# Down projections unit by unit, two-bank scores, a shorter last norm, and low parts of the first mixer's weights on VectorE

## The chip, the cores and the metric

The kernel runs on one core of a Trainium2 chip. The metric is device time in microseconds (us). Five engines work side by side, each in its own order of instructions: TensorE (PE: matmuls; PEld: its weight loads), VectorE (DVE), ScalarE (ACT), GpSimd (POOL) and SyncE (SP), which issues most of the transfers between device memory and the on-chip memory SBUF. Matmuls write PSUM, a small memory of eight banks, from which VectorE and ScalarE read.

## What is computed

The reference is a two-layer decoder trunk on one sequence of 1024 tokens with 1024 features, all in float32:

```python
def reference(x, ...):
    h = x
    for layer in range(DEPTH):                       # DEPTH = 2
        n = rms_norm(h, norm1_g[layer])
        if layer % 2 == 0:
            mix = retention_rwkv_mixer(n, ...)       # the first mixer: recurrences by chunks
        else:
            mix = swa_sink_mixer(n, ...)             # attention, 16 heads, window of 128
        h = h + mix
        n = rms_norm(h, norm2_g[layer])
        h = h + swiglu(n, ffn_w_gate[layer], ffn_w_up[layer], ffn_w_down[layer])
    return rms_norm(h, final_g)

def swiglu(h, w_gate, w_up, w_down):
    return (jax.nn.silu(h @ w_gate) * (h @ w_up)) @ w_down      # 1024 -> 2816 -> 1024
```

In attention, a block of 128 queries sees its own 128 keys and the 128 before them: scores, plus a band mask, a softmax with one learned extra term, and a weighted sum of values.

## The kernel before, in words

**Layout.** Features lie on the 128 partitions: `h` is 8 tiles of 128 features for each half of the tokens (`hf` 0 and 1, 512 tokens each, `HT`). A matmul has a 128x128 weight and 512 tokens.

**Three matmuls for one.** A float32 product is made of three faster ones. Each operand is split into a high part (a rounding cast on ScalarE) and a low part (operand minus high part, a subtraction on VectorE or GpSimd); then hi·hi, hi·lo and lo·hi are added in PSUM: `gemm` (L342-348) and, for the feed-forward part, `prod` (L1174-1179), where L1177, L1178 and L1179 are the three matmuls. The splits are `wsplit` (weights; cast L331, subtraction L332 on the engine `self.lo`, which is GpSimd unless set otherwise), `split` (activations; L352 cast, L354 subtraction) and `vsplit` (weights of the down projection; cast L1350, subtraction on GpSimd L1351). So no product starts before both parts of its weights and inputs are there. Split weights go through six buffers (`w` four, `wr` two).

**Who sets the order.** The kernel is written as a program over tiles. A scheduler then sets the order of the instructions on each engine, by its own model of their times; instructions that are given to `keep` hold their place in the program's order on their engine. Buffers come from named pools with a fixed number of each; a tile waits until the buffer's last user is done.

**The run.** First mixer with its output projection (a planner runs generators of jobs, `pl.run()`; for the first half of the tokens the weights are split and written back to memory, for the second the split weights are read), feed-forward part of layer 0, attention, feed-forward part of layer 1, final norm. The hidden features of the feed-forward part are made in 11 pairs of 256 (`NP`); a step of each pair ends in the gates (Silu on ScalarE, L1224) and the product with the up projection (L1228 on VectorE). Hidden tiles go to device memory (`hid`), and so do sums of them (`hc`), made by `form_down` (its `put` subtracts, L1304, splits and writes them).

**Down projection** (`down`, L1380 on). It is a two-by-two block product by seven products in place of eight (Strassen's way, in Winograd's form). In layer 0, 8 of the 11 pairs go through it in two groups of four slices (`DGROUPS`), the rest plainly; in layer 1 all 11 do, in groups of four, four and three. A group has seven stages s0 to s6. In a stage, one input X (hidden tiles, read from `hid` and split, or sums, read from `hc` split) meets four weights `W[dp]`, one for each of four PSUM banks: four units of 12 matmuls (9 in the group of three). Between them stand sums of weights (`wsum`: three for each `dp` in s0, one in s2) and additions of results to `h`, all on VectorE at L1377. Copies of results are at L1411 on ScalarE. The order of s0's units, the next input's split and the sums is the scheduler's. The first group's loads and splits come after the last pair of the feed-forward part has been written in program order, in pools (`fa`, `fz`) that open when the others close.

**Attention** (`attn`). 32 blocks of 128 queries for four heads at a time. The heads of a pair lie on partitions 0 to 63 and 64 to 127. For each row half `e`, two score matmuls (L1552, 64 rows of weights) go to a PSUM bank of their own, `r` or `c`, and VectorE adds the mask (L1556, 512 elements) into `s`; then maxima (L1562), exponentials on ScalarE (L1569), normalising (L1575), transposes on TensorE (L1582), copies (L1584 on ScalarE, L1586 on VectorE) and the product with the values (L1592). Projections of the feed-forward part (L346-348) run between.

**Final norm.** `final_r` (L1623 on): for each of the eight tiles a square and a copy scaled by the gain, both on ScalarE; sums of squares on VectorE (L1627) and over partitions by a matmul with ones (L1629); logarithm and exponential on ScalarE (L1631, L1632), each with a table load. `final_out` multiplies (L1639, VectorE and GpSimd) and writes the output (L1640). For the first half of the tokens `final_r` runs before the last two stages of the last group.

Of the kernel before, what the change touches and what calls it, by code (L numbers as in the profile page):

```python
# [13 lines left out]
ALU = mybir.AluOpType  # L14
# [190 lines left out]
class Kern:  # L205
    def __init__(self, ctx, tc, A, out):
# [15 lines left out]
        self.wx = None  # L222
        self.w6, self.nw, self.owed, self.lo = False, 0, [], self.nc.gpsimd
# [168 lines left out]
    def mixer0(self):  # L392
# [54 lines left out]
        jobs(1, "ret", (1, 2, 3))  # L447
        pl.run()
        gr.__exit__(None, None, None)
# [767 lines left out]
    def uses(self, L, p, sp, x=None):  # L1217
# [4 lines left out]
        def gate(nm, c):  # L1222
            sg[nm] = self.t(sp, [P, HT], "sg", 2) if nm == "11" else c
            S.activation(sg[nm], c, AF.Silu)  # L1224
# [61 lines left out]
    def ffn_pair(self, L, p, sp, next_w, form, x):  # L1286
# [10 lines left out]
        self.lockstep(*gens, form)  # L1297

    def form_down(self, L, p, x, ts):
# [3 lines left out]
        def put(i, o, a, b):  # L1303
            nc.vector.tensor_tensor(out=o, in0=a, in1=b, op=ALU.subtract)  # L1304
# [40 lines left out]
    def vsplit(self, v):  # L1345
# [4 lines left out]
        nc.scalar.copy(hi, v)  # L1350
# [29 lines left out]
    def down(self, L, fp, fz, rest, X=()):  # L1380


        op, S = self.vop, self.nc.scalar
        h0, h1 = (self.kt(self.h[hf]) for hf in range(2))
        dps = range(KT // 2)
        j = len(X)

        def place():
            nonlocal j
            i, j = j % (12 if L else 14), j + 1  # L1390
            if i >= 8 if L else i < 6:
                return self.t(fp, [P, 2, HT], "ha", 4 if L else 6, F32R)
            return self.t(self.pp, [P, 2, HT], "n8", 8, F32R)

        def plain(hf, f):
            return self.plain8(L, hf, f, place(), self.t(fp, [P, HT], "hr", 4))

        for g in DGROUPS[L]:
            n, ps = g[1] - g[0], range(*g)
            s1, u0 = [], []  # L1400
            W = [self.wdown(L, 0, g, fp, "wd0", 5)]
            X = X or [plain(0, 2 * p) for p in ps]
            W += [self.wdown(L, 2 * i, g, fp, "wd0", 5) for i in (1, 2, 3)]
            for i in dps:
                W[i] += self.wdown(L, 2 * i + 1, g, fp, "wd1", 6 - L)
            A = [self.pst(t, [P, HT]) for t in "fffy"]
            for dp in dps:
                a11, a12, a21, a22 = W[dp]
                self.prod(A[dp], self.vsplit(a11), X, True, False)
                u0.append(self.t(fz, [P, HT], "u0", 4))  # L1410
                S.copy(u0[dp], A[dp])  # L1411
                s1.append(op(self.wsum(fp, n, 4, 8), a21, a22))
                op(a21, a11, a21, ALU.subtract)
                W[dp][0] = op(self.wsum(fp, n, 4, 8), s1[dp], a11, ALU.subtract)
            X = [self.sums8(L, p, 2, place()) for p in ps]
# [18 lines left out]
            for _ in rest:  # L1434
                pass
# [398 lines left out]
```

## Time and profile before

| what | value |
|---|---|
| time, median of 3 runs | 2391.7 us (2388.97 to 2393.98) |
| the profiled execution | 2394.0 us, of which the span from first to last instruction is 2392.2 us |
| mean granted TensorE clock | 0.992 |
| TensorE busy | 2318.9 us (97%) |
| VectorE, GpSimd, ScalarE busy | 1626.3, 1193.1, 1025.5 us (68, 50, 43%) |
| down projection of layer 0, 1140 to 1340 us | TensorE 194.4 of 200 us busy, VectorE 134.3, GpSimd 139.8 |
| down projection of layer 1, 2140 to 2380 us | TensorE 231.0 of 240 us busy, VectorE 175.6, GpSimd 160.9 |

A row of the timeline gives the start, the duration, the engine, the line and operation, the tile written and those read, and a count; what stands in brackets is the engine's idle time before it and the instruction that ended the idle time. A row "x4" is four instructions in a row, with their time together. A row of a window gives its length, the busy time (and count) of PE, PEld, DVE, ACT and POOL, the granted clock, the DMA engines' busy share and GB/s. A row of groups gives busy time in all and mean ns of one, then the idle time before them and what ended it. A row of waits gives time in all, how often, and the longest. Matmuls are pipelined: each record is longer than the distance to the next, so their pace is read from start to start.

### The profile page before, as it was taken

How to read it: one execution, taken by the hardware profiler on the slowest of the kernel's cores; microseconds unless marked ns; L12 is line 12 of the kernel's file. 1: busy time of each engine (PE TensorE's matmuls, PEld its weight loads, DVE VectorE, ACT ScalarE, POOL GpSimd, SP SyncE). 2: the span in 40 equal slices, each digit the busy share in tenths (PEclk: the TensorE clock that was granted, in tenths of full speed). 3: DMA queues.
4: the chain of work that ended last, by engine and by line, in shares of the span. 5: the costliest groups of instructions: out<-in, count | busy, mean ns of one | idle time of the engine just before them, and what ended most of it. 6: DMA issues, size and time to landing. Idle time of an engine off the chain costs nothing. (4 is left out here: it accounts for less than half of the span.)

```text
span 2392.2 us, 35667 instructions
## 1 busy us (share of the span) xinstructions
PE 2318.9 (97%) x13098; PEld 1828.7 (76%) x13098; DVE 1626.3 (68%) x2462; ACT 1025.5 (43%) x1890; POOL 1193.1 (50%) x975
## 2 busy tenths in 40 slices
PE   8999899999999999999999999999999999999997
PEld 6776677777777888888778877677788788887785
DVE  5865855765567368885775469458638778887776
ACT  5354443324456333333333555455645233333336
POOL 7555331211541057776676632342232677767666
PEclk9999999999999999999999999999999999999999
DMA  7655454443445556563564321231336466547652
GB/s 267 197 204 188 154 165 133 126 128 115 146 172 181 198 171 212 195 216 137 217 222 153 118 62 58 66 131 62 106 128 220 159 217 218 203 178 274 219 200 107
DMA packets 167742, 395.93 MB, mean 166 GB/s; under 512 B 42896, under 2 KB 45584, under 8 KB 167568
## 3 DMA queue, kind: packets, MB, share of 16 engines
q1 hardware_dynamic: 164448, 388.15, 47.8%
q10 hardware_dynamic: 2832, 4.45, 0.6%
q8 instruction: 104, 1.70, 0.3%
q0 software_dynamic: 288, 1.05, 0.1%
q14 instruction: 70, 0.57, 0.1%
HBM read 271.29 MB, written 116.92 MB: 162 GB/s over the span
## 5 line engine op out<-in xcount | busy, mean ns | idle before, releaser
L332 POOL TENSOR_TENSOR w<-wr,w 128x512 fp32r<-128x512 f32 x196 | 264.3, 1354 | 427.9 <-ACT w L331 369.9
L239 PE MATMUL ps_f<-n,w 128*128 128x512 f32 x1440 | 383.5, 414 | 12.0 <-ACT w L331 6.4
L239 PEld LDWEIGHTS ps_f<-n,w 128*128 128x128 f32 x1440 | 268.3, 192 | 93.3 <-issue 21.9
L331 ACT CAST w<-wr 128x512 fp32r<-128x512 f32 x244 | 147.9, 612 | 188.8 <-PE ps_f L348 76.9
L332 POOL TENSOR_TENSOR w<-wq,w 128x512 fp32r<-128x512 f32 x92 | 130.5, 1430 | 31.7 <-ACT w L331 27.4
L346 PE MATMUL ps_f<-n,w 128*128 128x512 f32 x356 | 140.8, 396 | 2.6 <-ACT n L352 1.6
L347 PE MATMUL ps_f<-n,w 128*128 128x512 f32 x356 | 142.6, 400 | 0.0
L348 PE MATMUL ps_f<-n,w 128*128 128x512 f32 x356 | 140.1, 394 | 0.0
L1177 PE MATMUL ps_f<-n,w 128*128 128x512 f32 x322 | 127.5, 397 | 4.1 <-DVE h L1377 1.8
L1184 DVE TENSOR_TENSOR nq<-ps_m,u 128x512 f32<-128x512 f32 x88 | 58.7, 684 | 106.7 <-PE ps_m L1179 106.7
L1178 PE MATMUL ps_f<-n,w 128*128 128x512 f32 x322 | 125.5, 390 | 0.0
L1179 PE MATMUL ps_f<-n,w 128*128 128x512 f32 x322 | 125.2, 390 | 0.0
L354 POOL TENSOR_TENSOR n<-nq,n 128x512 fp32r<-128x512 f32 x64 | 106.0, 1667 | 10.2 <-ACT n L352 10.2
L1177 PE MATMUL ps_m<-n,w 128*128 128x512 f32 x282 | 110.6, 393 | 0.0
L1179 PE MATMUL ps_m<-n,w 128*128 128x512 f32 x282 | 109.8, 389 | 0.0
L1178 PE MATMUL ps_m<-n,w 128*128 128x512 f32 x282 | 109.8, 389 | 0.0
L332 POOL TENSOR_TENSOR wx<-wr,wx 128x512 fp32r<-128x512 f32 (+1 forms) x38 | 49.4, 1301 | 105.5 <-ACT wx L331 105.5
L1177 PE MATMUL ps_m<-cb,w 128*128 128x512 f32 x240 | 93.5, 389 | 0.9 <-DVE nq L1184 0.9
L1178 PE MATMUL ps_m<-cb,w 128*128 128x512 f32 x240 | 93.4, 389 | 0.0
L1179 PE MATMUL ps_m<-cb,w 128*128 128x512 f32 x240 | 93.4, 389 | 0.0
L1351 POOL TENSOR_TENSOR w<-wd,w 128x512 fp32r<-128x512 f32 (+1 forms) x53 | 75.9, 1442 | 32.0 <-ACT w L1350 31.8
L346 PEld LDWEIGHTS ps_f<-n,w 128*128 128x128 f32 x356 | 66.9, 188 | 20.0 <-ACT n L1598 2.2
(520 smaller groups left out, 6447.6 us busy)
## 6 DMA issues: line engine op xcount, KB each, us to landing
hc<-n SPq DMA_DIRECT2D x74, 512.0 KB, 2.7
wsp<-w SPq DMA_DIRECT2D x54, 512.0 KB, 3.4
w<-wsp SPq DMA_DIRECT2D x54, 512.0 KB, 3.7
wq<-in_w_gate SPq DMA_DIRECT2D x44, 512.0 KB, 4.2
u<-u SPq DMA_DIRECT2D x88, 256.0 KB, 2.9
n<-hc SPq DMA_DIRECT2D x43, 512.0 KB, 5.1
wr<-in_w_in SPq DMA_DIRECT2D x34, 512.0 KB, 5.0
hid<-n SPq DMA_DIRECT2D x66, 256.0 KB, 2.0
```

Source lines behind the costliest of these rows:

```text
L239: i = self.nc.tensor.matmul(out, lhsT, rhs, **kw)
L331: nc.scalar.copy(hi[:, :n], raw[:, c])
L332: self.lo.tensor_tensor(out=lo[:, :n], in0=raw[:, c], in1=hi.bitcast(F32)[:, :n], op=ALU.subtract)
L346: nc.tensor.matmul(ps, hi, rh, start=k == 0, stop=False)
L347: nc.tensor.matmul(ps, hi, rl, start=False, stop=False)
L348: nc.tensor.matmul(ps, lo, rh, start=False, stop=k == n - 1)
L354: e.tensor_tensor(out=lo, in0=src, in1=hi.bitcast(F32), op=ALU.subtract)
L1177: mm(ps, hi, xh, start=first and k == 0, stop=False, skip_group_check=True)
L1178: mm(ps, hi, xl, start=False, stop=False, skip_group_check=True)
L1179: mm(ps, lo, xh, start=False, stop=last and k == len(w) - 1, skip_group_check=True)
L1184: add = lambda o, x, y: V.tensor_tensor(out=o, in0=x, in1=y, op=ALU.add)
L1351: nc.gpsimd.tensor_tensor(out=lo, in0=v, in1=hi.bitcast(F32), op=ALU.subtract)
```

## The change

**Down projections.** `down` is written anew as one sequence of units (stage, `dp`). For each unit the program has: what follows the unit before (`post`), the split of a weight three units ahead (`ready`), a piece of the next stage's input (`prep`), the sums (`sums`), the transfers of an input two stages ahead (`get`) and, in s3 and s5, the loads of the next group's weights. The instructions of these on VectorE and ScalarE are held in that order (`pin`). All low parts in it are made on VectorE (`halves`): 139 of weights and 53 of hidden tiles; 25 of the latter were on VectorE before. One, the first weight's of layer 1, stays on GpSimd.

**The way in.** The last step of the last pair of the feed-forward part is put off (`rest(last)`). In layer 0 the first loads, the first input's splits and the first weights' come ahead of it; in layer 1 the first weight's load and split do. The pool `fa` opens earlier for it. In layer 1 the last `form_down` runs at the end of s2 of the first group (it stood ahead of its sums).

On ScalarE at the way into layer 0's down projection, with gates `ACTIVATE nq` and `u`, hidden tiles `hr` into `ha` and weights `wd` into `w` and `wr`, there stood:

```order
L1224 ACTIVATE nq_10326<-nq_10326 128x512
L1224 ACTIVATE u_1527_10317<-u_1527_10317 128x512
L1224 ACTIVATE nq_10325<-nq_10325 128x512
L1350 CAST wr_10534<-wd_1543_10494 128x512
L352 CAST ha_10496<-hr_10497 128x512
L352 CAST ha_10501<-hr_10502 128x512
L352 CAST ha_10506<-hr_10507 128x512
L352 CAST ha_10511<-hr_10512 128x512
L1350 CAST w_10556<-wd_1552_10516 128x512
```

and now (L1424 is the cast in `halves`, L1228 the gate):

```order
L1228 ACTIVATE nq_10326<-nq_10326 128x512
L1424 CAST ha_10463<-hr_10464 128x512
L1424 CAST ha_10466<-hr_10467 128x512
L1424 CAST ha_10469<-hr_10470 128x512
L1424 CAST ha_10472<-hr_10473 128x512
L1424 CAST wr_10483<-wd_1543_10461 128x512
L1424 CAST w_10548<-wd_1553_10486 128x512
L1228 ACTIVATE u_1527_10317<-u_1527_10317 128x512
L1424 CAST w_10551<-wd_1554_10488 128x512
L1228 ACTIVATE nq_10325<-nq_10325 128x512
```

The four casts of hidden tiles and two of weights have moved ahead of the last two gates.

**Attention.** The scores of both row halves go to one tile of two banks (`rc`), the loop over the row half is the inner one, and one addition of 1024 elements takes the place of two of 512. On TensorE, two consecutive blocks of the first half of the tokens (`ps_r`, `ps_c` the scores, `ps_m` transposes, `ps_y` products with values, `ps_f` projections) stood so before:

```order
L1552 MATMUL ps_r_13141<-ks_1861_12217,q_1876_12306 128x256 x2
L1552 MATMUL ps_c_13145<-kc_1856_12181,q_1876_12306 128x256 x2
...
L1582 MATMUL ps_m_13014<-c_ident_150,s_12988 128x128 x4
L1552 MATMUL ps_r_13186<-ks_1861_12217,q_1876_12306 128x256 x2
L1582 MATMUL ps_m_13020<-c_ident_150,s_12988 128x128 x2
L1592 MATMUL ps_y_12893<-pT_12886,vt_12220 64x256 x2
L1582 MATMUL ps_m_13020<-c_ident_150,s_12988 128x128 x2
L1552 MATMUL ps_c_13190<-kc_1856_12181,q_1876_12306 128x256 x2
```

and a block stands so now (L1665 the scores, L348 and L350 projections, L1706 the product with values):

```order
L1706 MATMUL ps_y_13010<-pT_12997,vt_12228 64x256 x3
L350 MATMUL ps_f_13549<-n_1843_12143,wx_13543 128x512
L1665 MATMUL ps_rc_13209<-ks_1861_12225,q_1876_12314 128x256
L1665 MATMUL ps_rc_13209<-kc_1856_12189,q_1876_12314 128x256
L1665 MATMUL ps_rc_13209<-ks_1861_12225,q_1876_12314 128x256
L1665 MATMUL ps_rc_13209<-kc_1856_12189,q_1876_12314 128x256
L348 MATMUL ps_f_13481<-n_1844_12144,w_13478 128x512
```

The four matmuls of a block stand together, the row halves in turn, where one block in the rows before had other work between them.

**First mixer.** While the planner runs, `wsplit` makes its low parts on VectorE: 66 instructions go there from GpSimd. VectorE's order near the start had additions `z` (L624) and the mixing with the token before (L627) right behind the norm (L463, L526):

```order
L463 SCALAR_TENSOR_TENSOR n_40_167<-r_22_137,pv_66,n_36_163 128x512
L526 TENSOR_TENSOR nq_204<-nq_201,nq_204 128x512
L624 TENSOR_TENSOR z_256<-ps_f_219,rs_237 128x512
L627 SCALAR_TENSOR_TENSOR wa_255<-wa_255,pv_66,z_256 128x512
L624 TENSOR_TENSOR z_297<-ps_f_271,rs_237 128x512
```

and has now low parts (L334) between them:

```order
L467 SCALAR_TENSOR_TENSOR n_40_167<-r_22_137,pv_66,n_36_163 128x512
L334 TENSOR_TENSOR w_263<-wr_139,w_263 128x512
L530 TENSOR_TENSOR nq_204<-nq_201,nq_204 128x512
L334 TENSOR_TENSOR w_266<-wr_139,w_266 128x512
L334 TENSOR_TENSOR w_305<-wr_269,w_305 128x512
L334 TENSOR_TENSOR w_309<-wr_269,w_309 128x512
L334 TENSOR_TENSOR w_347<-wr_313,w_347 128x512
L628 TENSOR_TENSOR z_256<-ps_f_219,rs_237 128x512
```

Five low parts of weights that TensorE uses for later tiles have come ahead of the first `z`.

**Final norm.** The scaled copies on ScalarE are gone; `final_out` multiplies by gain and factor in one instruction, always on VectorE. The logarithm's table is loaded in the stream, squares of the second half are made as its tiles are finished (`final_after`), and two of the first half's outputs are made in the last stage.

The diff, cut to its core:

```diff
+        self.lo = nc.vector
         pl.run()
+        self.lo = nc.gpsimd
...
-            S.activation(sg[nm], c, AF.Silu)
+            i = S.activation(sg[nm], c, AF.Silu)
+            if self.hold:
+                self.keep(i)
...
+    def pin(self, i):
+        k = str(i.ins.engine)
+        if k in self.pins:
+            self.tc.add_manual_dep(i.ins, self.pins[k], self.nosync, reason="order")
+        self.pins[k] = i.ins.name
+        return i
...
+        def halves(o, t, src):
+            pin(S.copy(t[0], src))
+            pin(V.tensor_tensor(out=t[1], in0=src, in1=t[0].bitcast(F32), op=ALU.subtract))
+            o.append((t[0], t[1]))
...
+        for i, (si, dp) in enumerate(units):
+            gi, s = gs(si)
+            if i:
+                k = self.done(post, L, *gs(units[i - 1][0]), units[i - 1][1])
...
+            while len(ready) < 3 and i + len(ready) < len(units):
+                u, v = units[i + len(ready)]
+                if gs(u)[1] == 0 or True:
+                    ready.append(split(part(*gs(u), v)))
+            if si + 1 < len(stages):
+                prep(si + 1, dp)
+            sums(gi, s, dp)
+            if i and k is not None:
+                self.final_after(k)
+            if self.outs and s == 6 and dp > 1:
+                next(self.outs)
+            if si + 2 < len(stages):
+                get(si + 2, dp)
+            if gi + 1 < len(DGROUPS[L]):
+                if s == 3:
+                    load(gi + 1, dp)
+                if s == 5:
+                    load(gi + 1, dp + 4)
+            if gi == 0 and s == 2 and dp == 3:
+                while self.owed:
+                    self.keep(self.nc.sync.dma_start(*self.owed.pop(0)))
+                for _ in rest:
+                    pass
+            ps = banks[gi, "ABABBCC"[s]][dp]
+            self.prod(ps, ready.popleft(), XS[si], s in (0, 1, 5), s in (2, 4, 6))
...
-                for e in range(2):
-                    ps = self.pst("rc"[e], [P, 2, 256])
...
+                ps = self.pst("rc", [P, 2, 2, 256])
+                for i in range(2):
+                    for e in range(2):
...
-            nc.scalar.activation(h(k), h(k), AF.Copy, scale=self.col("nf", k))
...
+                nc.vector.scalar_tensor_tensor(
+                    out=h(k), in0=h(k), scalar=self.col("nf", k), in1=r, op0=ALU.mult, op1=ALU.mult
+                )
...
+        last = ffn_late(0, sp, K.pp, opened)[3]
+        close(gb)
         gf, fp = K.pool("fa", "left")
+        fs = [fp]
+        f = K.down(0, fs, ())
+        next(f)
+        rest(last)
...
         r0 = K.final_r(0, fz, order[0], 7)
+        K.keep(tc.nc.scalar.preload_act_table(AF.Ln))
+        K.outs = K.final_out(0, r0, order[0])
         run(f)
-        r1 = K.final_r(1, fz, order[1], 4)
-        K.final_out(0, r0, order[0], "pppppppp")
-        K.final_out(1, r1, order[1], "vpvvpvvp")
+        r1 = K.final_r1(fz)
+        run(K.outs)
+        run(K.final_out(1, r1, order[1]))
```

259 lines of the change are left out of this document (174 added, 85 removed).

## The prediction

> **What bounds the kernel now.** I began with the page's busy times, then the windows of 20 and 30 us, then what TensorE waited for in each stage, and last the timeline at those waits.
>
> ```profile
> PE 2318.9 (97%) x13098; PEld 1828.7 (76%) x13098; DVE 1626.3 (68%) x2462; ACT 1025.5 (43%) x1890; POOL 1193.1 (50%) x975
> ...
> 2310.00:2340.00 30.00, 30.00 (x134) 24.86 (x133) 17.12 (x21) 13.70 (x26) 16.15 (x17) 1.00 0.55 184
> 1180.00:1200.00 20.00, 20.00 (x90) 16.56 (x89) 10.70 (x15) 4.35 (x7) 15.47 (x11) 1.00 1.02 390
> 0.00:300.00 300.00, 277.08 (x2129) 210.45 (x2130) 205.40 (x371) 141.48 (x225) 162.10 (x183) 0.98 0.60 202
> ```
>
> TensorE is busy for 97% of the span, and the change removes hardly any of its work, so a gain can only come from its holes and from the ends. Where nothing waits, 90 matmuls of 512 columns fill 20 us: one starts every 0.222 us. The two down projections are such stages with holes in them. These rows are TensorE's waits of 1140 to 1340 us (first five) and of 2140 to 2380 us (last five):
>
> ```profile
> PE ps_f L1178 <- POOL ha L354: 2.1, 1, 2.1
> PE ps_r L1177 <- ACT wr L1350: 1.4, 1, 1.4
> PE ps_y L1177 <- DVE h L1377: 1.1, 1, 1.1
> PE ps_f L1177 <- DVE h L1377: 0.6, 1, 0.6
> PE ps_m L1179 <- POOL wr L1351: 0.2, 1, 0.2
> ...
> PE ps_f L1177 <- DVE h L1377: 3.1, 3, 1.6
> PE ps_f L1179 <- POOL wr L1351: 1.8, 1, 1.8
> PE ps_y L1177 <- ACT w L1350: 0.9, 1, 0.9
> PE ps_f L1178 <- POOL ha L354: 0.8, 1, 0.8
> PE ps_f L1177 <- ACT w L1350: 0.7, 1, 0.7
> ```
>
> That is 5.4 us in layer 0 and 7.3 us in layer 1. The timeline at the first of them shows why:
>
> ```profile
> 1148.28 0.63 ACT L1224 ACTIVATE nq<-nq 128x512 f32<-128x512 f32 x1 [5.18 <-DVE nq L1184]
> ...
> 1149.33 2.17 ACT L352 CAST ha<-hr 128x512 fp32r<-128x512 f32 x4
> 1150.74 3.46 POOL L354 TENSOR_TENSOR ha<-hr,ha 128x512 fp32r<-128x512 f32 x2
> 1156.49 1.67 DVE L1377 TENSOR_TENSOR wd<-wd,wd 128x512 f32<-128x512 f32 x1
> 1159.78 0.68 DVE L1377 TENSOR_TENSOR ws<-wd 128x512 f32<-128x512 f32 x1
> 1168.50 0.63 PE L1177 MATMUL ps_m<-ha,wr 128*128 128x512 f32 x1
> ...
> 1171.06 0.63 PE L1179 MATMUL ps_r<-ha,wr 128*128 128x512 f32 x1
> ```
>
> ScalarE cannot cast the first halves before the last gate has run (1148.28 us), and only then does GpSimd begin its low parts at 1.73 us each (3.46 for two). Beside them the same kind of subtraction on VectorE takes 1.67 us instead of 0.68, so both chains are late for the second stage too. After such a hole TensorE goes at half pace for a while: the last two rows are the first and the last of seven matmuls that start (1171.06 − 1168.50) / 6 = 0.427 us apart, and layer 1 has seven such too; 7 × (0.427 − 0.222) = 1.4 us each. Measured from start to start, with 0.222 us taken off, all stops come to another 1.9 and 2.0 us, since a restart is slower than the wait shown and some stops are too short for the list. So the down projections lose 5.4 + 1.4 + 1.9 = **8.7 us** (layer 0) and 7.3 + 1.4 + 2.0 = **10.7 us** (layer 1).
>
> **Part 1: the way into the down projections.** In layer 0 the hid halves and first weights come ahead of the last gates, in layer 1 the first weight does. The casts then run while TensorE still has the last products to do, and VectorE makes a low part in 0.68 us. A unit of 12 matmuls lasts 12 × 0.222 = 2.67 us, and the low parts for the next one need 0.7 us each, so after the first unit VectorE keeps ahead. So the 2.1, 1.4 and 0.2 us of layer 0 go, and the 1.8 and 0.8 us of layer 1, with the slow clock after them. What is late next is the second stage's transfers, which are issued no earlier than now; what they may cost is in the residual below. In layer 1 VectorE has these on its way as well:
>
> ```profile
> 2152.85 1.64 DVE L1304 TENSOR_TENSOR n<-n,n 128x512 f32<-128x512 f32 x1
> ```
>
> Four such subtractions (some 6.6 us) stand ahead of the first sums now, and go to the end of the third stage. Their four splits and two transfers to memory go with them. They are needed only in the third group, more than one group of 75 us later, so this move is costed at nothing; if the transfers were late after all, the third group would wait. It puts 4 × 0.68 = 2.7 us on VectorE at that place, about one unit, out of a lead of two units.
>
> **Part 2: the steady down projections.**
>
> ```profile
> 2242.60 0.68 DVE L1377 TENSOR_TENSOR h<-h,ps_f 128x512 f32<-128x512 f32 x1
> 2243.20 0.68 DVE L1377 TENSOR_TENSOR ws<-wd,ws 128x512 f32<-128x512 f32 x1
> ```
>
> The waits on `h` (0.6, 1.1 and 3.1 us) are late writers of a PSUM bank behind the slow sums, and those on ACT `w` (0.9, 0.7) are casts that stood behind other waits. With GpSimd silent, VectorE's instructions should all take the 0.68 us of the row above. What VectorE then has to do: 92 instructions in a group of four slices, × 0.68 = 63 us, against 28 units × 2.67 = 75 us of TensorE. It fits. In the first two stages of a group it is 4 × 0.68 = 2.72 us against 2.67, which the lead absorbs. In the last group of layer 1 (three slices, units of 2.0 us, 56 us) it is about full: 28 low parts and 16 sums of 384 columns at 0.55, 9 hid halves, 36 additions and some 12 of the norm at 0.68, two outputs at 0.75: 24 + 39 + 1.5 = 64 us by durations. Back to back they start 0.60 us apart (the two rows above), so 64 × 0.60 / 0.68 = 57 us. New residual waits: between 0 (lead suffices) and 8 (64 − 56), taken at **+2.5 us**, nearer to 0 because durations overlap.
>
> **Part 3: the tail.**
>
> ```profile
> 2374.00 0.39 PE L1179 MATMUL ps_y<-n,wr 128*128 128x512 f32 x1
> ...
> 2378.17 1.28 ACT L1631 ACT_TABLE_LOAD   x1
> 2382.12 6.29 DVE L1639 TENSOR_TENSOR h<-h,y 128x512 f32<-128x512 f32 x5 [7.01 <-ACT y L1632]
> ...
> L1610 DVE SCALAR_TENSOR_TENSOR h<-h,pv,ps_f 128x512 f32<-128x512 f32 x8 | 6.0, 746 | 14.9 <-PE ps_f L348 14.9
> ```
>
> The last product ends at E = 2374.4 and the span at 2392.2: 17.8 us. Of this, 3.8 us lie behind the last multiplication (2382.12 + 6.29 = 2388.4). After the change the scaling copies and one table load are gone from this path, but 14 of 16 outputs are fused operations on VectorE alone. By the row above: E + 1.0 (last `h`) + 14 × 0.746 = 10.5 + 3.8 = E + 15.3; the factor of the second half comes in time: from the first table load to the multiplications it took 2382.12 − 2378.17 = 3.95 us, without one load 2.7, behind the last `h`, a square and two matmuls, so by about E + 5, while the first six outputs run until E + 5.5. Saving **2.5 us**; at worst 0 (transfers of the outputs end no sooner), at best 4.5 (more of them done in the stream).
>
> **Part 4: attention.**
>
> ```profile
> 1477.81 0.48 PE L1552 MATMUL ps_r<-ks,q 64*128 64x256 f32 x1
> 1477.82 0.48 PE L1552 MATMUL ps_c<-kc,q 64*128 64x256 f32 x1
> ...
> 1478.88 0.50 PE L347 MATMUL ps_f<-n,wx 128*128 128x512 f32 x1
> ...
> 1482.96 1.13 PE L1552 MATMUL ps_r<-ks,q 64*128 64x256 f32 x4
> 1485.33 1.13 PE L1552 MATMUL ps_c<-kc,q 64*128 64x256 f32 x4
> ...
> L1556 DVE TENSOR_TENSOR s<-ps_r,c_amask 128x512 f32<-128x512 f32 x28 | 19.0, 680 | 10.8 <-PE ps_c L1552 10.0 <-PE ps_r L1552 0.7
> L1562 DVE TENSOR_REDUCE st<-s 128x4 f32<-128x1024 f32 x28 | 33.9, 1212 | 0.2
> ...
> 1400.00:1420.00 20.00, 20.00 (x106) 14.69 (x107) 18.72 (x46) 12.49 (x41) 6.03 (x5) 1.00 0.14 40
> ```
>
> Where the two heads' score matmuls stand next to each other, `r` and `c` start 0.01 us apart and the block's eight records take 1.07 us; where the scheduler put other work between, 1.13 + 1.13 = 2.26. I find 9 of 32 blocks apart. The change makes nearly all adjacent: at most 9 × 1.19 = 11 us of TensorE. The new addition of 1024 elements isn't in the trace; by the reduction over as many (1.21) against two additions (1.36) it saves 0.15 us a block, 5 us in all. If it costs more than two, nothing is gained. About half of the 11 lies in the second half, where TensorE is the limit (5.5); in the first, VectorE is (18.7 of 20 us), so 16 × 0.15 = 2.4. One bank pair instead of two single banks makes the next scores wait for the one addition: I take off 2. **−6 us**, between −2 and −11.
>
> The Trainium skill (TensorE: Matmul & The Clock Gate, Part 3, The mechanism) says that matmuls stay in program order and only weight loads are pulled ahead. By it, the order r r c c of before could not overlap as these rows show, and alternating them would pay in all 32 blocks. The trace disagrees: the adjacent block already starts r and c together.
>
> **Part 5: the first mixer.**
>
> ```profile
> L332 POOL TENSOR_TENSOR w<-wr,w 128x512 fp32r<-128x512 f32 x64 | 88.2, 1385 | 45.9 <-ACT w L331 43.6 <-DVE z L624 1.8
> 30.85 2.72 PE L239 MATMUL ps_f<-n,w 128*128 128x512 f32 x7 [1.27 <-POOL w L332]
> 260.00:280.00 20.00, 18.52 (x148) 14.55 (x148) 18.58 (x52) 5.60 (x9) 5.51 (x7) 0.83 0.24 86
> 280.00:300.00 20.00, 16.87 (x97) 12.62 (x97) 19.27 (x37) 13.36 (x20) 10.07 (x8) 0.95 0.59 191
> ```
>
> 66 low parts go from GpSimd (1.39 us each) to VectorE: 66 × 0.68 = 45 us onto 205 of 300 us, less what its other instructions get back when GpSimd stands beside them less. That leaves it under (205 + 45) / 300 = 84% there, and a low part takes half as long. The 1.27 us wait on GpSimd goes, with some of the slow clock behind it; in the full stretch 260 to 300 us the added work costs something back. **−2 us**; bounds −8 (a third of the 23 us of holes) and +44 (rival C).
>
> **Sum.** −8.7 − 10.7 + 2.5 − 2.5 − 6 − 2 = −27.4 us. The profiled execution took 2394.0 us (span 2392.2 and 1.8 around it), so **2366.6 us**. It lies 2.3 us above the median of the three runs (2391.7), which differ by 5 among themselves; I leave that in the range.
>
> **Rivals.** *B, VectorE becomes the limit of the down projections.* For it: 64 us of durations against 56 in the last group, 2.72 against 2.67 in the first stages, and pinned orders on two engines. Against it: the 0.60 us spacing. Then the residual is 8 in the last group and about 2 in each of the three or four other groups' first stages, 14 instead of 2.5: 2378. The Trainium skill (Perfetto Trace Analysis, Optimizing Scalar/DVE Operations) advises the opposite move, off VectorE when it is saturated, while warning that shifting work between it and GpSimd may not help since they share a read port; the 1.67 against 0.68 us agrees with the warning.
>
> *D, attention and tail give nothing* (VectorE sets the pace there, and the pair of banks takes back what adjacency gives): 2394 − 19.4 + 2.5 − 2 = 2375.
>
> *C, slower: the mixer's VectorE queue is held by low parts.* It runs in order. A low part at its head waits for its cast, and what is queued behind, the additions and chain steps of the recurrence, waits too, and TensorE for them. GpSimd idled 43.6 us for casts in these rows; with the 45 us of work that is 89 us, and 205 + 89 = 294 of 300. If half of it falls ahead of a step that TensorE awaits: 2394 − 25.4 + 44 = 2413. From 25 us on it outweighs the rest. Against it: VectorE is 68% busy, casts come early.
>
> *E, the alternation pays in all 32 blocks:* 32 × 1.19 = 38 instead of 6, 2335. The rows at 1477.8 speak against it. The rule of the Trainium skill in part 4 would have it so.
>
> *F, the pinned order doesn't bring the first halves forward*, and the holes stay but are shorter: half of 19.4 lost: 2376 at best, 2387 with D: no change that can be told.
>
> **Chances.** Forecast 0.55, B 0.18, D 0.11, C 0.09, F 0.06, E 0.01. A difference under 0.2% (4.8 us) cannot be told from none. Faster: 0.55 + 0.18 + 0.11 + 0.01 and a third of F, 0.87; same 0.04; slower 0.09. The range reaches down to 2354 (attention −11, mixer −8 and no residual together would be 2394 − 19.4 − 2.5 − 11 − 8 = 2353) and up to 2386, which holds B, D and most of F.
>
> **What would show it.** Right: no wait of TensorE over 0.5 us at the start of either down projection, no 0.43 us spacing there; VectorE's instructions at 0.68 us all through; the span ends 15 us after the last product; score blocks of 1.1 us throughout; TensorE's busy time of the first 300 us not lower. Wrong: waits on VectorE low parts in the first two stages or the last group (B); a first mixer that ends later, with TensorE waiting for low parts or chain steps on VectorE (C).

## The result, and the profile after

The changed kernel takes 2365.6 us (median of 5 runs, 2361.9 to 2370.1) against 2391.7 (5 runs, 2388.3 to 2394.0). The ratio is 0.9884, with a 95% interval of 0.9868 to 0.9901. The forecast was 2366.6 us. The total is right, but partly by luck: some of its terms are wrong in opposite directions, and two of its reasons do not hold. A table of stages shows which. Its edges are single matmuls that both traces have, so it adds up to the spans:

| stage, up to | before | after | difference | forecast |
|---|---|---|---|---|
| last gate product of the first mixer | 673.0 | 676.2 | +3.2 | −2 |
| first product of layer 0's down projection | 477.0 | 476.7 | −0.3 | |
| first score of attention | 236.9 | 228.1 | −8.8 | −8.7 |
| last norm before layer 1's feed-forward part | 400.4 | 385.3 | −15.1 | −6 |
| last product ahead of layer 1's down projection | 363.6 | 365.5 | +1.9 | |
| start of the last product | 223.1 | 213.6 | −9.5 | −10.7 |
| end of the span | 18.2 | 18.5 | +0.3 | −2.5 |
| sum | 2392.2 | 2363.9 | −28.3 | −27.4, with 2.5 of residual waits |

How far can a row be trusted? The kernels below share most stages with the changed one. In ten profiles with the same first mixer it took 670.6 to 683.0 us; in ten with the same attention 385.3 to 387.9; in thirteen with the same feed-forward code in layer 1, 363.6 to 365.5; in eight with the same layer 1 down projection 212.9 to 213.6. So the differences in attention and the down projections are well clear of this scatter, the +1.9 is within it, and the first mixer makes up most of the scatter between whole runs. The 673.0 us of before, one profile, lies inside the ten's range (their mean is 676.2), so the +3.2 is not clear of it either.

The page's busy times of the kernel after:

```profile
PE 2301.2 (97%) x13092; PEld 1820.3 (77%) x13092; DVE 1656.5 (70%) x2677; ACT 1008.2 (43%) x1872; POOL 854.8 (36%) x731
```

GpSimd's 1193.1 us have become 854.8, VectorE's 1626.3 only 1656.5: what came to it, 2677 instructions in place of 2462, was mostly paid by shorter instructions (in the first 300 us the norm's products, L463 before and L467 after, went from a mean of 1002 ns to 744). TensorE's waits from 2128 to 2347 us in it, the down projection of layer 1 (in layer 0 it has none):

```profile
PE ps_r L1183 <- DVE w L1425: 0.8, 1, 0.8
PE ps_f L1181 <- ACT w L1424: 0.7, 1, 0.7
```

and two windows, the first 300 us of the first mixer and layer 0's down projection:

```profile
0.00:300.00 300.00, 277.28 (x2128) 210.03 (x2129) 212.72 (x412) 140.44 (x224) 83.20 (x120) 0.97 0.61 205
1140.00:1340.00 200.00, 200.00 (x883) 165.38 (x882) 148.96 (x220) 76.41 (x137) 34.07 (x28) 1.00 0.54 191
```

Of twelve waits in the down projections of before, two are left, 1.5 us instead of 12.7; in layer 0 TensorE is busy 200 of 200 us where it was 194.4. The first wait that is left comes from VectorE, at the place to which the last `form_down` was moved (starts, durations, engines as in the timelines of before):

```profile
2167.93 1.78 DVE L1310 TENSOR_TENSOR nq<-n 128x512 f32<-128x512 f32 x1
...
2170.23 1.18 DVE L1425 TENSOR_TENSOR w<-wd,w 128x512 fp32r<-128x512 f32 x1
...
2171.46 0.50 PE L1183 MATMUL ps_r<-n,w 128*128 128x512 f32 x1 [0.75 <-DVE w L1425]
```

The four subtractions are followed by splits whose low parts are GpSimd's; beside two of those the last subtraction takes 1.78 us and a weight's low part 1.18, and TensorE waits for that low part.

The tail, where 2.5 us were expected:

```profile
2345.40 0.39 PE L1183 MATMUL ps_y<-n,wr 128*128 128x512 f32 x1
...
2347.06 0.74 DVE L1777 SCALAR_TENSOR_TENSOR h<-h,pv,y 128x512 f32<-128x512 f32 x1
2347.72 0.68 DVE L1420 TENSOR_TENSOR h<-h,ps_y 128x512 f32<-128x512 f32 x1
2349.06 3.68 PE L1766 MATMUL ps_m<-nq,c_ones 128*128 128x512 f32 x4 [3.27 <-DVE nq L1758]
...
2355.44 5.39 DVE L1777 SCALAR_TENSOR_TENSOR h<-h,pv,y 128x512 f32<-128x512 f32 x8 [2.46 <-ACT y L1769]
```

The last `h` starts 2.3 us after the last product has started, behind an output; TensorE stands idle for 3.27 us and then takes 3.68 us for two matmuls with ones; the factor is there 10 us after the last product, and VectorE has been idle for 2.46 us by then.

The first mixer's start, ScalarE's cast, VectorE's `z` and TensorE (after):

```profile
27.76 1.14 ACT L333 CAST w<-wr 128x512 fp32r<-128x512 f32 x2 [9.69 <-DMA wr<-in_w_in]
30.21 0.69 ACT L476 ACTIVATE rs<-ps_m,c_eps 128x512 f32<-128x512 f32 x1
...
32.72 0.63 ACT L477 ACTIVATE rs<-rs 128x512 f32<-128x512 f32 x1
...
33.38 0.69 DVE L628 TENSOR_TENSOR z<-ps_f,rs 128x512 f32<-128x512 f32 x1 [1.25 <-ACT rs L477]
34.13 2.50 PE L241 MATMUL ps_f<-n,w 128*128 128x512 f32 x5 [5.84 <-DVE z L628]
```

ScalarE waits 9.69 us for a transfer of weights, and the norm's factor `rs`, whose sums were there at 25.3 us, is queued behind that cast. Before, its last step ran 7.5 us earlier:

```profile
25.18 0.63 ACT L473 ACTIVATE rs<-rs 128x512 f32<-128x512 f32 x1
```

And attention, first the group of the new addition:

```profile
L1669 DVE TENSOR_TENSOR s<-ps_rc,c_amask 128x1024 f32<-128x1024 f32 x28 | 34.0, 1215 | 6.5 <-PE ps_rc L1665 6.4
```

and the first two of a block's scores in the timeline:

```profile
1574.47 0.48 PE L1665 MATMUL ps_rc<-kc,q 64*128 64x256 f32 x1
1574.48 0.48 PE L1665 MATMUL ps_rc<-ks,q 64*128 64x256 f32 x1
```

The addition takes 1.215 us; the estimate by the reduction row was 1.21. The two row halves start 0.01 us apart, as in the adjacent block of before.

### The profile page after: what moved, and what is told of

It is laid out like the page before. It is cut to its first block, busy times and chain, and to the rows that moved or that the text cites. A ratio compares the mean times of both kernels' runs of the same rounds, so it can differ in the third digit from the quotient of the medians.

```text
span 2363.9 us, 35505 instructions
## 1 busy us (share of the span) xinstructions
PE 2301.2 (97%) x13092; PEld 1820.3 (77%) x13092; DVE 1656.5 (70%) x2677; ACT 1008.2 (43%) x1872; POOL 854.8 (36%) x731
## 4 chain that ended last, share of the span: by engine, by line
PE 79%; DVE 10%; ACT 4%; DMA 3%; issue 2%; SPq 1%; POOL 1%; DVEq 0%; ACTq 0%; POOLq 0%
PE ps_f L241 9%; PE ps_m L1181 7%; PE ps_m L1183 7%; PE ps_m L1182 7%; PE ps_f L349 5%; PE ps_f L348 5%; PE ps_f L350 5%; PE ps_m L241 5%; PE ps_f L1181 4%; PE ps_f L1182 4%; PE ps_f L1183 4%; PE ps_c L1183 2%; PE ps_c L1182 2%; PE ps_c L1181 2%; PE ps_r L1183 2%
## 5 line engine op out<-in xcount | busy, mean ns | idle before, releaser
L241 PEld LDWEIGHTS ps_f<-n,w 128*128 128x128 f32 x1440 | 269.4, 193 | 97.5 <-issue 21.0
L334 POOL TENSOR_TENSOR w<-wr,w 128x512 fp32r<-128x512 f32 (+1 forms) x130 | 175.0, 1351 | 376.6 <-ACT w L333 323.5
L334 POOL TENSOR_TENSOR w<-wq,w 128x512 fp32r<-128x512 f32 x92 | 130.4, 1429 | 37.1 <-ACT w L333 28.1
L348 PE MATMUL ps_f<-n,w 128*128 128x512 f32 x356 | 141.4, 397 | 2.1 <-ACT n L354 1.6
L350 PE MATMUL ps_f<-n,w 128*128 128x512 f32 x356 | 140.2, 394 | 0.0
L334 DVE TENSOR_TENSOR w<-wr,w 128x512 fp32r<-128x512 f32 x114 | 81.1, 714 | 42.4 <-ACT w L333 42.3
L333 ACT CAST w<-wq 128x512 fp32r<-128x512 f32 x92 | 55.9, 619 | 65.7 <-PE ps_m L1183 53.9
L334 POOL TENSOR_TENSOR wx<-wr,wx 128x512 fp32r<-128x512 f32 (+1 forms) x38 | 50.0, 1314 | 90.9 <-ACT wx L333 90.9
```

Of the source, the lines that this page charges most:

```text
L241: i = self.nc.tensor.matmul(out, lhsT, rhs, **kw)
L333: nc.scalar.copy(hi[:, :n], raw[:, c])
L334: self.lo.tensor_tensor(out=lo[:, :n], in0=raw[:, c], in1=hi.bitcast(F32)[:, :n], op=ALU.subtract)
L348: nc.tensor.matmul(ps, hi, rh, start=k == 0, stop=False)
L350: nc.tensor.matmul(ps, lo, rh, start=False, stop=k == n - 1)
```

## The experiments

Each kernel is the changed one with the edit shown. "Stage" figures are the rows of the table above, from the profile of the run. Of all these kernels, only a_old has a ratio whose interval lies clear of the changed kernel's (0.9868 to 0.9901); the other readings rest on stages and waits in one profile each, set beside the scatter given above.

**m_gpsimd.** The first mixer's low parts on GpSimd again:

```diff
-        self.lo = nc.vector
         pl.run()
```

> The changed kernel with the first mixer's low parts back on GpSimd, the rest as changed. The changed kernel reached the end of the first mixer 3.2 us later than before and TensorE waited 5.8 us for a VectorE addition z at 34 us. Theory S (the start: on ScalarE two casts that wait for a transfer now stand ahead of the norm's logarithm, so the factor rs and with it z come 7.5 us later): 2362 us, 3 to 4 less than the changed kernel, and no wait on z. Rival V (VectorE's added 45 us cost time all through the mixer): also 2362. Rival N (an accident of the order elsewhere): 2366, no change. This run tells N from the others, the next one S from V.

2363.4 us (0.9896 of before, 0.9872 to 0.9919). The wait on `z` is gone (a wait of 2.2 us on a GpSimd low part stands there), which speaks against N. The mixer takes 672.2 us, inside the range of the ten, and the run's time doesn't differ clearly from the changed kernel's.

**m_start.** Only the first 14 low parts on GpSimd, the other 52 on VectorE:

```diff
+        self.lo, self.early_lo = nc.vector, 14
         pl.run()
...
+            e, self.early_lo = (nc.gpsimd if self.early_lo > 0 else self.lo), self.early_lo - 1
```

> The changed kernel with only the first 14 low parts of the first mixer on GpSimd, the other 52 on VectorE as changed. ScalarE's and VectorE's order up to some 40 us is then that of the kernel before. Theory S: the wait of 5.8 us goes, 2361 to 2362 us. Rival V: at most a fifth of the loss goes (14 of 66), 2365 us.

2358.5 us (0.9867, 0.9852 to 0.9881), the fastest of all; the mixer takes 667.7 us. Its four runs (2357.8 to 2362.1 us) lie below the four of d_gates_first on the same chip (2362.3 to 2371.0), which is the changed kernel over again, as told there. ScalarE and TensorE in it:

```profile
25.05 0.63 ACT L479 ACTIVATE rs<-rs 128x512 f32<-128x512 f32 x1
26.06 1.14 ACT L334 CAST w<-wr 128x512 fp32r<-128x512 f32 x2 [0.38 <-DMA wr<-in_w_in]
...
30.70 3.06 PE L242 MATMUL ps_f<-n,w 128*128 128x512 f32 x12 [2.21 <-POOL w L336]
```

The factor is computed ahead of the casts, at 25.05 us, and the wait of 5.84 us is a wait of 2.21. Theory S holds for the wait: it comes from ScalarE's order at the start. All ten profiles with 66 low parts on VectorE have this wait (5.7 to 7.5 us); the three with fewer (m_gpsimd, m_start and `best`) have one of 2.1 to 2.2 us on a GpSimd low part instead. The mixer's mean is 676.2 us in the ten and 670.6 in these three. V fell: 52 low parts on VectorE did not lengthen the mixer.

**d_gpsimd.** The down projections' low parts on GpSimd, order unchanged:

```diff
-            pin(V.tensor_tensor(out=t[1], in0=src, in1=t[0].bitcast(F32), op=ALU.subtract))
+            pin(self.nc.gpsimd.tensor_tensor(out=t[1], in0=src, in1=t[0].bitcast(F32), op=ALU.subtract))
```

> The changed kernel with the low parts of both down projections on GpSimd, in the same order by units. If it is the low parts' engine that made the 18 us in the down projections (sums beside GpSimd 1.67 us instead of 0.68, low parts 1.3 to 1.7 us): 2374 us or more, with waits on GpSimd low parts and sums of 1.7 us. If it is the order by units with splits three ahead: 2366 to 2368 us.

2369.2 us (0.9911, 0.9894 to 0.9928). Neither expectation: layer 0's stage is 228.2 us, as in the changed kernel, without a single wait, and layer 1's 218.7, 5.1 more, while the tail is 2.7 shorter. The groups in the two down projections (first two rows layer 0, third layer 1):

```profile
L1425 POOL TENSOR_TENSOR w<-wd,w 128x512 fp32r<-128x512 f32 x21 | 32.6, 1569 | 16.2 <-ACT w L1424 16.2
L1420 DVE TENSOR_TENSOR ws<-wd,ws 128x512 f32<-128x512 f32 x8 | 10.7, 1334 | 0.0
...
L1420 DVE TENSOR_TENSOR ws<-ws,wd 128x512 f32<-128x512 f32 x8 | 12.0, 1506 | 0.0
```

and TensorE's longer waits in layer 1:

```profile
PE ps_f L1181 <- DMA ha<-hc: 2.4, 3, 1.6
...
PE ps_y L1181 <- DVE h L1420: 0.8, 1, 0.8
PE ps_r L1181 <- ACT wr L1424: 0.7, 1, 0.7
```

VectorE's sums are as slow as ever beside GpSimd, 1.3 to 1.5 us, and the low parts take 1.57. In layer 0 nothing of it reaches TensorE. The engine of the low parts matters in layer 1 only, and there nearly half of the waits (2.4 of 5.5 us) are for inputs that land late.

**d_gates_first.** Layer 0's last gates written ahead of the down projection's first loads:

```diff
+        rest(last)
         f = K.down(0, fs, ())
         next(f)
-        rest(last)
```

> The changed kernel with the last gates of layer 0 ahead of the down projection's first loads and splits, as before; low parts stay on VectorE. If the order of the casts at the way in matters: a hole of 1.5 to 2.5 us and slow matmuls behind it at the start of layer 0's down projection, 2368 to 2369 us. If the faster low parts alone suffice: within 1 us of the changed kernel, 2366 us.

2365.5 us (0.9895, 0.9877 to 0.9914), stage 227.9. This tells nothing of the gates: the scheduler put the casts ahead of them all the same, and no engine's order differs from that of the changed kernel. So it is that kernel measured again, and shows its scatter: the first mixer takes 683.0 us here and 676.2 there. The next kernel holds the order.

**d_gates_pinned.** The same, and the gates held in ScalarE's order:

```diff
             if self.hold:
-                self.keep(i)
+                self.pin(i)
```

> The changed kernel with the last three gates of layer 0 held ahead of the down projection's first casts in ScalarE's order, as before (the run before this one left ScalarE's order as changed). If the earlier casts make the gain at layer 0's way in: a hole of 1.5 to 2.5 us with slow matmuls behind it, 2.5 to 4 us more from the first product of the down projection to the first score (228.0 in the changed kernel, 236.9 before). If low parts on VectorE and the order by units suffice: 228 to 229.

2368.7 us (0.9911, 0.9889 to 0.9933). The first product comes behind a wait; from the first mixer's end to attention's first score it takes 707.8 us in place of 704.8. ScalarE and TensorE at the place:

```profile
1147.87 0.63 ACT L1229 ACTIVATE nq<-nq 128x512 f32<-128x512 f32 x1 [5.18 <-DVE nq L1189]
1148.40 2.16 ACT L1426 CAST ha<-hr 128x512 fp32r<-128x512 f32 x4
1150.47 0.62 ACT L1426 CAST wr<-wd 128x512 fp32r<-128x512 f32 x1
...
1151.14 0.50 PE L1182 MATMUL ps_f<-ha,wr 128*128 128x512 f32 x1 [1.69 <-ACT wr L1426]
...
1153.39 0.50 PE L1184 MATMUL ps_f<-ha,wr 128*128 128x512 f32 x1 [0.48 <-DVE wr L1427]
```

With the gate first, casts start at 1148.4 and TensorE waits 1.69 and 0.48 us, 3.0 us with the restarts. The early casts are worth 3 us of layer 0's gain. Of the holes behind the first stage (1165 to 1172 us and 1228 to 1233 us before), none came back.

**d_two.** One unit less of lead:

```diff
-            while len(ready) < 3 and i + len(ready) < len(units):
+            while len(ready) < 2 and i + len(ready) < len(units):
```

> The changed kernel with the weights of the down projections split one unit less ahead (two in hand in place of three, the running one counted). With low parts on GpSimd layer 0 had no wait either, so the theory is now that the order by units with its lead removes the waits. If the lead matters: waits of 0.5 us and more return, 3 us or more in the two down projections (213.6 us from the end of the feed-forward products to the last product in layer 1). If one unit of 2.67 us is lead enough for a low part of 0.7 us: within 1 us.

2367.6 us (0.9901, 0.9882 to 0.9921). Layer 0's stage is 230.5 (+2.4), layer 1's 219.4 (+5.8), the tail 15.3 (−3.3). TensorE's longer waits, in layer 0 (first row) and in layer 1:

```profile
PE ps_f L1181 <- ACT w L1424: 0.9, 2, 0.6
...
PE ps_m L1183 <- DVE w L1425: 2.5, 1, 2.5
PE ps_f L1181 <- ACT w L1424: 1.4, 1, 1.4
PE ps_y L1181 <- ACT w L1424: 0.7, 1, 0.7
```

One unit of lead is worth 8.2 us in the two down projections. Part of that comes back in the tail, where TensorE's idle time ahead of the matmuls with ones is 1.7 us in place of 3.3 and these run at 0.43 us a record; why VectorE comes through sooner there was not tried.

**a_old.** The scores as before, in two single banks, with the row half as the outer loop and two additions:

```diff
+                for e in range(2):
+                    ps = self.pst("rc"[e], [P, 2, 256])
+                    a = slice(64 * e, 64 * e + 64)
+                    src = (kc if e == rg else ks)[ti]
+                    for i in range(2):
...
-                ps = self.pst("rc", [P, 2, 2, 256])
```

> The changed kernel with the scores as before: two tiles of one bank, row halves one after the other, two additions of 512 elements. The attention stage (from the first score to the last projection) went from 389.8 to 374.6 us, 15 less, where 6 were forecast. If all of this is the edit's: 2380 to 2381 us. If the forecast's 6 was right and the rest is an accident of the scheduler's order: 2371 to 2372 us.

2380.3 us (0.9942, 0.9925 to 0.9959; before took 2394.9 on this chip), the stage 401.6 us: 15 more than the ten profiles with the changed attention (385.3 to 387.9). All of the gain is the edit's, with the order that the scheduler makes of it.

**a_two_adds.** Adjacent scores in one tile of two banks, two additions of 512 elements:

```diff
+                for e in range(2):
+                    V.tensor_tensor(
+                        out=s.rearrange("p (i e) k -> p e i k", e=2)[:, e, :, kw], in0=ps[:, e, :, kw],
+                        in1=amask[:, kw].rearrange("p (o t) -> p o t", o=1).to_broadcast([P, 2, nk]), op=ALU.add,
+                    )
```

> The changed kernel with the scores of both row halves adjacent in one two-bank tile, but with two additions of 512 elements in place of one of 1024. If the gain comes from adjacent score matmuls on TensorE: within 3 us of the changed kernel, 2366 to 2368 us. If it comes from VectorE's shorter work: the addition of 1024 elements takes 1.2 us against two of 0.68, 0.15 us a block and 5 us over 32 blocks, so 2370 us or more.

2371.8 us (0.9900 of 2394.9, 0.9886 to 0.9915), the stage 392.5 us: 9.1 less than a_old, which is what adjacent scores give while both additions stay, and 4.6 to 7.2 more than the ten profiles with one addition. The group of the additions:

```profile
L1670 DVE TENSOR_TENSOR s<-ps_rc,c_amask 128x512 f32<-128x512 f32 x56 | 35.9, 680 | 5.8 <-PE ps_rc L1665 5.8
```

A block's additions take 2 × 0.680 = 1.36 us against 1.215, 0.145 us more, 4.6 us in 32 blocks. The size fits, the place does not. Each half of the tokens has 16 blocks. The table splits the stage at the norms' matmuls with ones (L371 in the kernel after) behind the first half's blocks and ahead of the second's; the 38.3 us between them are the same in all:

| stretch of the attention stage | before | a_old | the ten | a_two_adds | a_rows_in_turn |
|---|---|---|---|---|---|
| first half's blocks | 132.7 | 133.8 | 127.3 to 129.8 | 127.3 | 129.5 |
| second half's blocks, to the end | 229.4 | 229.5 | 219.7 | 226.9 | 223.9 |

In the first half the second addition costs nothing. In the second half the stage loses 7.2 us, where the additions grow by 16 × 0.145 = 2.3. The scheduler ordered the rest of attention anew in this run, and the next run, with VectorE's work unchanged, loses 4.2 us in the same place. So adjacency has some 8 to 10 of the 15; how the remaining 5 to 7 divide between VectorE's shorter work and the order is open.

**a_rows_in_turn.** The four matmuls of a block in the order r r c c:

```diff
-                for i in range(2):
-                    for e in range(2):
+                for e in range(2):
+                    for i in range(2):
```

> The changed kernel with the four score matmuls of a block in the order r r c c in place of r c r c, still adjacent, still one addition. By the trace of before, where r r c c ran side by side when adjacent: no change, 2364 to 2367 us, a block's scores in 1.07 us. By the rule of the Trainium skill (TensorE: Matmul & The Clock Gate, Part 3, matmuls stay in program order) only the middle two could overlap: some 0.5 us or more a block, 16 us, so 2380 us or more.

2373.6 us (0.9905 of a before of 2394.9 on this chip, 0.9886 to 0.9924), the stage 391.7 us. The first four score records of one block on TensorE:

```profile
1430.87 0.48 PE L1665 MATMUL ps_rc<-ks,q 64*128 64x256 f32 x1
1430.89 0.48 PE L1665 MATMUL ps_rc<-kc,q 64*128 64x256 f32 x1
1431.19 0.38 PE L1665 MATMUL ps_rc<-ks,q 64*128 64x256 f32 x1
1431.21 0.38 PE L1665 MATMUL ps_rc<-kc,q 64*128 64x256 f32 x1
```

The halves still start 0.02 us apart. From start to start, all score matmuls take 35.3 us, against 33.6 in the changed kernel and 43.5 in a_old. So the rule by which only the middle two could overlap does not hold here. The stage is 4 to 6 us longer all the same, so the time lies between the two expectations: 1.7 of it are the scores, 2 to 3 the transposes. The scheduler moved other instructions of attention too; what each of them costs, this run doesn't tell.

**t_outs_after.** No output in the last stage:

```diff
-            if self.outs and s == 6 and dp > 1:
-                next(self.outs)
```

> The changed kernel with no output made in the last stage: all eight of the first half come behind the last sums of squares. In the changed kernel the last h came 2.6 us after the last product in place of 1.0, with two outputs of 0.74 us ahead of it on VectorE. If they delay the second half's factor, which sets the end: the factor comes 1.5 us earlier and VectorE has no idle time before the last eight, 2364.3 us. If VectorE's sum of work sets the end: no change or up to 1.5 us more, 2366 to 2367 us.

2365.2 us (0.9875 of 2394.9, 0.9857 to 0.9893). The end behind the last product's start takes 17.0 us in place of 18.5, as expected if the outputs delay the factor, which comes 1.5 us earlier. But VectorE still idles 0.97 us before the last eight, and the median shows no gain over the changed kernel.

**t_warm.** TensorE kept busy behind the last product:

```diff
+            mmi = self.prod(ps, w, XS[si], s in (0, 1, 5), s in (2, 4, 6))
+        if L:
+            pin(mmi)
+            self.wps = self.pst("m", [P, HT])
+            for _ in range(self.nwarm):
+                pin(self.nc.tensor.matmul(self.wps, w[0][0], XS[-1][0][0], start=True, stop=True))
```

> The changed kernel with 16 matmuls more, of no use, right behind the last product, so that TensorE is busy until the sums of squares are there; result unchanged. In the changed kernel TensorE idles 3.3 us there and the two matmuls with ones then take 3.7 us, against 4.45 us for five such in before. If the idle time halves the clock: 1.8 to 2.0 us for the two, and an end 1.5 to 1.8 us earlier behind the last product (18.5 us now). If they are slow for another reason, 3.7 us and no change.

2364.5 us (0.9888, 0.9870 to 0.9906). TensorE at the end (last product, the 16 added matmuls, the matmuls with ones):

```profile
2344.26 0.39 PE L1184 MATMUL ps_y<-n,wr 128*128 128x512 f32 x1
2344.48 3.79 PE L1569 MATMUL ps_m<-n,wr 128*128 128x512 f32 x16
2348.11 1.88 PE L1774 MATMUL ps_m<-nq,c_ones 128*128 128x512 f32 x4
```

1.88 us in place of 3.68, and the span ends 16.9 us behind the start of the last product (2361.2 − 2344.3) in place of 18.5. It was the idle time that made them slow. Its length alone does not decide it, though. The same four records behind shorter idle times, in t_outs_after and d_gpsimd:

```profile
2352.45 3.51 PE L1764 MATMUL ps_m<-nq,c_ones 128*128 128x512 f32 x4 [1.95 <-DVE nq L1756]
...
2355.46 1.98 PE L1766 MATMUL ps_m<-nq,c_ones 128*128 128x512 f32 x4 [2.25 <-DVE nq L1758]
```

After 1.95 us they are slow, after 2.25 us they are not; what decides, no run here shows. The 1.6 us are seen in the profile; in the runs' medians they are lost in the scatter.

**best.** m_start, t_outs_after and t_warm together.

> Three edits together: the first 14 low parts of the first mixer on GpSimd, the first half's outputs behind the last sums, and the 16 matmuls that keep TensorE busy. By the parts: 7 less (mixer) and 1.5 to 3 less (end) than the changed kernel's 2365.6: 2356 us. If the parts do not add up, since the last eight outputs on VectorE set the end: 2358 us.

2361.4 us (0.9876, 0.9858 to 0.9893): above both expectations, and no better than m_start alone. Its mixer took 671.9 us in the profile where m_start's took 667.7 with the same mixer code, and its end again 16.9 us behind the last real product: the two edits of the tail do not add up. With outputs late, the sums are there at 2345.3 us but the ones' matmuls wait for the 16 added ones until 2346.8.

## Why the prediction was right, and where it was not

**The down projections: right in size, partly right in cause.** The early casts took the 2.1 us wait away; d_gates_pinned puts 3 us on them. But the second stage's waits (1.4 and 0.2 us, with the slow matmuls) and those on `h` did not go because "with GpSimd silent, VectorE's instructions should all take the 0.68 us". d_gpsimd has GpSimd as loud as before, sums of 1.3 us, and no wait in layer 0. That step failed: the new order is enough in layer 0, and d_two, with one unit less of lead, has 2.4 us of waits again there. What the rest of the order does (the sums in their units, the earlier transfers) was not taken apart. The low parts' engine is worth 5 us, in layer 1 alone, and 2.7 of that come back in the tail. Layer 1's row came out 1.3 us better than −10.7 + 2.5; its holes in before come to some 11.3 us from start to start, so they were priced a little low.

**The residual: right.** Forecast +2.5 us, measured 2.7 in layer 1, start to start over 0.222 us: stops of 1.0 and 1.1 us with their restarts at 2171 and 2341 us, and 0.6 more between 2174 and 2178. Its place was in part the one costed "at nothing": the moved subtractions took 0.68 to 1.78 us each, since GpSimd makes the low parts of their results beside them, and the lead was used up there. Rival B came true in that small form only.

**The tail: wrong.** Forecast −2.5, measured +0.3. The step that failed is "the factor of the second half comes in time ... by about E + 5": it came at E + 9.65, with E the end of the last product (2345.79 us in the kernel after). Three things make up the 4.65 us. Two outputs stand in VectorE's order ahead of the last `h`, which ends at E + 2.6, not E + 1.0 (t_outs_after: 1.5 us). TensorE's idle time makes the matmuls with ones take 3.7 us where they take 1.9 when it is kept busy (t_warm: 1.6 us). And the sum left 1.3 us for a square and two matmuls that take 0.66 + 1.88 = 2.5 even so. Each of the first two alone takes the tail to 17 us; `best`, with both, stays at 16.9, so mending both did not reach the forecast's 15.7 (18.2 − 2.5).

**Attention: right mechanism, size off.** The scores fell from 43.5 us to 33.6, start to start: 9.9 of the 11 forecast as the upper end. I had halved that, taking VectorE as the limit of the first half, and had taken 2 off for the shared pair of banks. The step that failed is that limit: the first half's blocks lost 5.4 us (132.7 to 127.3), and giving VectorE its second addition back costs nothing there (a_two_adds). In the second half the scores fell from 23.2 to 17.2 us and the transposes from 19.1 to 14.9, which I had not priced. Over the stage, transposes and products with values fell by some 9 us between the two traces, and the projections rose by 3.5. How much of that is VectorE's shorter work and how much the scheduler's order is open.

**The first mixer: no gain, and not for the rival's reason as priced.** Forecast −2, measured +3.2 in one profile, which lies within the scatter. The step that failed is "the 1.27 us wait on GpSimd goes": it went, but a wait of 5.84 us came in its place. Rival C had VectorE's low parts hold the chain. What held it is one step further on: the scheduler, given the new low parts, put two casts that await a transfer ahead of the norm's logarithm on ScalarE, and `z` and TensorE waited behind them, 5.8 us. The rest of the mixer shows no harm: in m_start it was shorter than in any other profile. That it gains from 52 low parts on VectorE is not shown, since `best`, with the same mixer, took 671.9, m_gpsimd 672.2 and before 673.0.

Two slips in the sums changed nothing: (205 + 45) / 300 is 83%, not 84, and rival F with D comes to 2394 − 9.7 + 2.5 − 2 = 2385, not 2387; either would have been told from 2394 by the 4.8 us that the prediction itself gives.

That the total came within 1 us was luck: errors of −9 (attention), +5 (mixer, much of it scatter) and +3 (tail) nearly cancelled.

## What to carry to other kernels

Give each producer a lead of some units in a fixed order before moving it to a faster engine: here the order removed the waits of layer 0's down projection while the producers stayed slow (d_gpsimd). Read a moved instruction's queue on every engine, not only its own: a new low part on VectorE changed ScalarE's order, and the cost was there. When an edit's undoing shows no difference, look whether the instructions really moved (d_gates_first) before concluding.

## What the hardware showed beside

Adjacent matmuls on 64 rows each, one from partitions 0 to 63 and one from 64 to 127, run side by side even when issued r r c c (starts 0.02 us apart; 35.3 us for all scores, 43.5 where 9 of 32 blocks are kept apart). After 3.3 us without work TensorE takes 0.92 us a record for a float32 matmul with ones where it takes 0.47 when kept busy; after 1.95 us it was slow as well, after 2.25 us in another run it was not. One addition of 1024 elements out of two PSUM banks takes 1.215 us, two of 512 elements 1.36. A subtraction with both operands in SBUF takes 0.68 us on VectorE alone and up to 1.8 us beside one of GpSimd's (1.67 and 1.78 us in the rows shown), in the kernel after as before.
